# A new opening for a two-layer trunk kernel: sums of squares as columns, k tiles 0 to 2 in another order, tiles declared ahead

## The chip, the cores and the metric

The kernel runs on one core of one Trainium2 chip. It is one program for five engines: TensorE (PE; its weight loads are shown apart as PEld), VectorE (DVE), ScalarE (ACT), GpSimd (POOL) and SyncE (SP), which issues nearly all loads. The metric is device time in microseconds (us) of one execution, as a median over runs. A profiled execution has a span, from its first to its last instruction, and its own time, which also holds what lies around the span.

## The reference

Two layers work on 256 latent positions and 256 context positions, each 2048 wide, all in float32. Each layer normalises its input, scales and shifts it with vectors made from a conditioning vector, multiplies by one wide matrix, mixes three groups of columns in different ways, and multiplies by an output matrix. The opening of layer 0 is what matters here:

```python
def rmsnorm(x, g):
    xf = x.astype(jnp.float32)
    y = xf * lax.rsqrt(jnp.mean(xf * xf, axis=-1, keepdims=True) + EPS)
    return (y * g.astype(jnp.float32)).astype(x.dtype)

for l in range(DEPTH):
    shift, scale, gate = jnp.split(silu_c @ w_mod[l] + b_mod[l], 3, axis=-1)
    shift_c, scale_c, gate_c = jnp.split(silu_cc @ w_mod[l] + b_mod[l], 3, axis=-1)
    h = rmsnorm(x, g_pre[l]) * (1.0 + scale[:, None]) + shift[:, None]
    h_c = rmsnorm(ctx, g_pre[l]) * (1.0 + scale_c) + shift_c
    proj = h @ w_in[l]
    proj_c = h_c @ w_in[l]
    ...
```

## The kernel before

Latents and context lie side by side as 512 columns, and the 2048 features as 16 tiles of 128 partitions, the k tiles. For k tile 0 the order is: the sum of squares of the latents over all features, then its power -1/2, then that row spread over all partitions, then shift and scale of the tile (`mod_start`), then h for the latents (`make_h`), and only then the first products of the wide matrix. The context follows in the same steps while PE works on the latents.

A product in full precision is made of three in the fp32r form: weights and h are each split into a high part (a cast on ACT) and a low part (a subtraction on DVE), and `mm3` adds high x high, high x low and low x high. Weights come through three `raw` tiles and are split by `W.emitting(cut)` in pieces of `cut` columns, a cast and a subtraction for each; a load into a `raw` tile waits until the subtraction that read its old content is done. Tiles are handed out by tag, each tag with a fixed number of places that are used in turn.

The first sums (lines 1282 to 1300): ACT squares a loaded tile that holds two k tiles (128x512), PE multiplies it with 32 columns of ones (line 1286; four such products share one bank in four strips of partitions), ACT copies the 128x512 result (line 1291), four narrow products add the strips up and turn the row into columns (line 1295), DVE scales (line 465), POOL raises to the power (line 468), and `bcast` spreads it (line 489). `warm` issues idle matmuls (line 483).

`mod_start` makes shift and scale of one k tile: 16 products over 2 MB of loaded weights (line 169), a transpose on DVE (line 173), four small products (line 178, `modc`) and three small DVE instructions (lines 187 to 190). Its weights go by turns into two sets of tiles (mraw, macc, vv and mg, mgl, hh14 to hl15). `next(...)` and `mod_in` do one step of it, so the loop decides where each step stands. For each k tile the loop in `layer` issues four groups of av products (`start_av`; groups 0 and 1 are latents, 2 and 3 context) and two or three of au (`start_au`). Head 2 of au, called au2 here, has weights of its own, which stand in hh12, hl12, hh13 and hl13. Up to k tile EARLY the modulation of the next tile stands inside the iteration (early form); later tiles have it one tile further ahead, with modc right behind the 16 products (late form).

In this first stage the order on PE, DVE, ACT and SP is the order in which the code issues (`manual_schedule`); each engine works strictly through its list and waits where an operand isn't ready. SP's loads wait in the same way, for the tile they write to come free and for their turn.

Of the kernel before, what the change touches and what calls it, by code (L numbers as in the profile page):

```python
# [7 lines left out]
F32 = mybir.dt.float32  # L8
# [5 lines left out]
P = 128  # L14
# [52 lines left out]
def trunk_kernel(ctx: ExitStack, tc: tile.TileContext, xT, xhalf, cT, wss, wsl, wmod, win, wout0, wout1, const, vec, rows,  # L67
# [66 lines left out]
    gg0 = sb([P, KT, 2], F32, "gg0")  # L134
    g1 = []

    def mod_cols(l, cb, ps8):
# [145 lines left out]

    LOADS = [0, 2, 0, 2, 1, 1, 1, 1, 1, 0, 2, 0, 1, 1, 1, 0]
    SPLITS = [1, 1, 0, 2, 0, 1, 1, 1, 1, 1, 0, 2, 0, 1, 1, 1]
    EARLY = 7
    LOWC = 60
    YT = 3.0
    GATES = {2: 0, 14: 1}, {7: 2}, {12: 3}, {}
# [53 lines left out]
    class Stream:  # L343
# [247 lines left out]
    def layer(l):  # L591
# [43 lines left out]
        if l == 0:  # L635
# [8 lines left out]
            for k in range(KT):  # L644
                def take_in(n):
                    mod_in(k + 1, n)
# [8 lines left out]
                        mod_in(k + 1)  # L655
                        make_h(0, k + 1, rb0, [0, 1])

                if k == 2:
                    ws_[0] = ahead
                elif k % 2 == 0:  # L660
                    take(k)
                if 0 < k <= EARLY:
                    take_in(1)
                if k == 1:
                    next(state["load"])
                if k >= EARLY:
                    mod_in(k + 2, 1)
                for _ in range(LOADS[k]):
# [1 line left out]
                if k == 0:  # L670
# [3 lines left out]
                    au.extend(mm_ps("au") for _ in range(2))  # L674
                    take_in(2)
                    make_h(0, 0, rb0[:, CTX], [1])
                    take_in(1)
                    e = W.emitting(512)
                    next(e)
                    take_in(1)  # L680
                    next(e)
                    next(state["w0"])
                    start_av(0, (2,))
                    mod_in(1)
                    start_av(0, (3,))
                    make_h(0, 1, rb0, [0, 1], state["w0"])
                    take(0, (1,))
                    start_au(0, (0, 1))
                elif k == 1:
                    au.append(ms_ps("au"))  # L690
                    start_av(1, (0, 1))
                    take_in(5)
                    avs = W.emitting(512)
                    next(avs)
                    start_av(1, (2,))
                    take_in(1)
                    start_av(1, (3,))
# [553 lines left out]
    with tc.manual_schedule(engines={EN.PE}):  # L1251
# [27 lines left out]
        idle = mm_ps("idle")  # L1279
        rb0 = sb([P, T], F32, "acc")  # L1280

        def square(sq, s, i):
            q = w2k([P, T])
            A.activation(q, yo[2 * i + s], AF.Square)
            c = slice(32 * (i % 4), 32 * (i % 4) + 32)
            return lambda: PE.matmul(sq[c], ones[:, 0:32], q, start=i < 4, stop=i >= 4,
                                     tile_position=(0, 32 * (i % 4)))

        def sums_of(sq):
            row = w2k([P, T])  # L1290
            A.copy(row, sq)
            ps = ms_ps("rs")
            for j in range(2):
                for i in range(2):
                    PE.matmul(ps[:, j:j + 1], row[:, (2 * i + j) * P:(2 * i + j + 1) * P], cc("sel")[:, 0:1],
                              start=i == 0, stop=i == 1)
            return rstd_cols(ps[:, 0:2], 2, D)

        def spread(r, s):
            rb = bcast(r, 2)  # L1300
# [3 lines left out]
        for i in range(8):  # L1304
# [15 lines left out]
        warm(idle, 2)  # L1320
        sq = mm_ps("rs2")
        products = [square(sq, 1, i) for i in range(2)]
        list(m)
        warm(idle, 3)
        make_h(0, 0, rb0[:, LAT], [0])
        state["w0"] = e

        def context(between):
            products.extend(square(sq, 1, i) for i in range(2, 8))
            for p in products:  # L1330
                p()
            r = sums_of(sq)
            between()
            spread(r, 1)

# [83 lines left out]
```

## Time and profile before

| What | Value |
|---|---|
| Time, median of 3 runs | 1139.67 us (1139.26 to 1140.7) |
| Profiled execution, its own time | 1140.22 us |
| Its span | 1138.4 us |
| PE busy in the span | 1123.5 us, 99% |
| DVE, ACT, POOL busy | 880.6, 515.1, 34.6 us |
| Mean granted PE clock | 0.998 |

A row of the timeline gives start, length, engine, line, operation, output and inputs, shapes and a count of merged records; in brackets stands how long the engine had stood idle and what ended that. In a row of busy time by stretch each engine has its busy time and record count, in the order PE, PEld, DVE, ACT, POOL; then come the granted PE clock, the DMA engines' busy share and GB/s.

### The profile page before, as it was taken

The page shows a single profiled execution, that of the slowest core. Times are in us where ns is not written, and L with a number is a line of the kernel's source. Part 1 is how long each engine was busy: PE and PEld are TensorE (multiplying, and loading weights), DVE is VectorE, ACT ScalarE, POOL GpSimd, SP SyncE. Part 2 cuts the span into 40 slices and gives each one's busy share as a digit, 9 for nine tenths or more (in the row PEclk, how much of TensorE's full clock was granted, in tenths as well). Part 3 has the DMA queues.
Part 4 walks back from the last instruction along what each step waited for, and adds up shares of the span by engine and source line. Part 5 has one row for each costly group of instructions (what it writes and reads, how often), then busy time and mean ns, then how long its engine had stood idle before and what let it go on. Part 6 is the DMA issues. An engine that isn't in the chain of part 4 may idle for free.

```text
span 1138.4 us, 16831 instructions
## 1 busy us (share of the span) xinstructions
PE 1123.5 (99%) x6323; PEld 930.7 (82%) x6323; DVE 880.6 (77%) x1484; ACT 515.1 (45%) x938; POOL 34.6 (3%) x40
## 2 busy tenths in 40 slices
PE   8999999999999999999999999999999999999997
PEld 3667788888898888888888888988888988888885
DVE  1645499999987887789999994397788689868884
ACT  5322422222325667632533323365555369857551
POOL 0000000000000000000000000205000000000001
PEclk9999999999999999999999999999999999999999
DMA  9999756556655343355556665269656686555872
GB/s 351 404 379 405 254 187 189 176 194 212 212 167 185 111 136 117 116 188 186 165 190 215 213 197 162 63 187 236 209 179 210 213 274 193 175 164 191 294 260 74
DMA packets 72946, 234.28 MB, mean 206 GB/s; under 512 B 8480, under 2 KB 11424, under 8 KB 72864
## 3 DMA queue, kind: packets, MB, share of 16 engines
q1 hardware_dynamic: 70416, 231.10, 61.1%
q0 software_dynamic: 2304, 2.10, 1.2%
q8 instruction: 49, 0.80, 0.3%
q14 instruction: 33, 0.27, 0.1%
q10 hardware_dynamic: 144, 0.02, 0.0%
HBM read 231.08 MB, written 2.10 MB: 205 GB/s over the span
## 4 chain that ended last, share of the span: by engine, by line
PE 90%; DVE 5%; DMA 2%; ACT 1%; issue 1%; POOL 0%; SPq 0%; DVEq 0%; POOLq 0%; ACTq 0%
PE ps_t L437 13%; PE ps_t L439 13%; PE ps_t L438 13%; PE ps_t L559 10%; PE ps_t L560 5%; PE ps_y L437 3%; PE ps_y L439 3%; PE ps_y L438 3%; PE ps_mod L169 2%; PE ps_av L437 2%; DVE macc L207 2%; PE ps_av L438 2%; PE ps_av L439 2%; PE ps_tp L952 2%; PE ps_v L439 1%; PE ps_v L437 1%
## 5 line engine op out<-in xcount | busy, mean ns | idle before, releaser
L412 ACT CAST whi<-raw 128x1024 fp32r<-128x1024 f32 (+1 forms) x217 | 224.2, 1037 | 327.4 <-PE ps_t L438 186.4
L417 DVE TENSOR_TENSOR wlo<-raw,whi 128x1024 fp32r<-128x1024 f32 (+1 forms) x217 | 260.7, 1206 | 57.6 <-ACT whi L412 54.8
L437 PE MATMUL ps_t<-hh,whi 128*128 128x512 f32 (+1 forms) x704 | 268.6, 382 | 0.0
L439 PE MATMUL ps_t<-hh,wlo 128*128 128x512 f32 (+1 forms) x704 | 268.1, 381 | 0.0
L438 PE MATMUL ps_t<-hl,whi 128*128 128x512 f32 (+1 forms) x704 | 267.9, 381 | 0.0
L207 DVE SCALAR_TENSOR_TENSOR macc<-mraw,cs,macc 128x512 f32<-128x512 f32 x360 | 249.3, 746 | 17.9 <-DMA mraw<-in_wmod_dram 17.7
L559 PE MATMUL ps_t<-hh,whi 128*128 128x512 f32 x448 | 163.5, 402 | 0.0
L439 PEld LDWEIGHTS ps_t<-hh,wlo 128*128 128x128 f32 x704 | 132.3, 188 | 25.9
L437 PEld LDWEIGHTS ps_t<-hh,whi 128*128 128x128 f32 x704 | 132.5, 188 | 25.2 <-issue 0.8
L438 PEld LDWEIGHTS ps_t<-hl,whi 128*128 128x128 f32 x704 | 132.4, 188 | 24.1
L560 PE MATMUL ps_t<-hh,wlo 128*128 128x256 f32 x448 | 125.6, 280 | 0.0
L559 PEld LDWEIGHTS ps_t<-hh,whi 128*128 128x128 f32 x448 | 84.2, 188 | 19.0 <-issue 0.5
L560 PEld LDWEIGHTS ps_t<-hh,wlo 128*128 128x128 f32 x448 | 84.7, 189 | 0.5 <-issue 0.5
L525 ACT ACTIVATE hh<-w2k,sh 128x256 fp32r<-128x256 f32 x48 | 21.9, 502 | 76.4 <-DVE w2k L521 76.4
L437 PE MATMUL ps_y<-whi,hh 128*128 128x512 f32 x104 | 41.4, 398 | 0.0
L437 PE MATMUL ps_av<-whi,hh 128*128 128x512 f32 x96 | 40.0, 416 | 0.8 <-ACT hh L525 0.8
L439 PE MATMUL ps_y<-whi,hh 128*128 128x512 f32 x104 | 40.7, 392 | 0.0
L438 PE MATMUL ps_y<-wlo,hh 128*128 128x512 f32 x104 | 40.6, 390 | 0.0
L437 PE MATMUL ps_cx<-whi,hh 128*128 128x512 f32 x96 | 38.8, 404 | 0.0
L438 PE MATMUL ps_av<-wlo,hh 128*128 128x512 f32 x96 | 37.8, 393 | 0.0
L438 PE MATMUL ps_cx<-wlo,hh 128*128 128x512 f32 x96 | 37.4, 390 | 0.0
L454 ACT CAST w2k<-ps_tp 128x512 fp32r<-128x512 f32 x40 | 23.3, 583 | 23.2 <-PE ps_scc L438 12.7
(397 smaller groups left out, 1858.0 us busy)
## 6 DMA issues: line engine op xcount, KB each, us to landing
raw<-in_win_dram SPq DMA_DIRECT2D x158, 512.0 KB, 4.3
mraw<-in_wmod_dram SPq DMA_DIRECT2D x128, 512.0 KB, 4.4
raw<-in_wout_dram SPq DMA_DIRECT2D x60, 512.0 KB, 4.4
mraw<-in_wsl_dram SPq DMA_DIRECT2D x16, 512.0 KB, 7.1
yo<-in_xhalf_dram SPq DMA_DIRECT2D x16, 256.0 KB, 5.4
macc<-in_wsl_dram SPq DMA_DIRECT2D x8, 512.0 KB, 7.7
vv<-in_wsl_dram SPq DMA_DIRECT2D x8, 512.0 KB, 7.7
mg<-in_wsl_dram SPq DMA_DIRECT2D x8, 512.0 KB, 6.6
```

The source lines that it names most:

```text
L169: PE.matmul(ps[32 * kk:32 * kk + 32, 0:n], cpad[:, kg * 4 + kk], ws[kk], start=kg == 0, stop=kg == 3, tile_position=(0, 32 * kk))
L207: V.scalar_tensor_tensor(out=acc[:, s], in0=w[:, kk % 2], scalar=c, in1=acc[:, s], op0=ALU.mult, op1=ALU.add)
L412: A.copy(ph, rc)
L417: self.last = V.tensor_tensor(out=pl, in0=rc, in1=ph.bitcast(F32), op=ALU.subtract)
L437: PE.matmul(ps, st[0], mv[0], start=start, stop=False)
L438: PE.matmul(ps, st[0], mv[1], start=False, stop=False)
L439: PE.matmul(ps, st[1], mv[0], start=False, stop=stop)
L454: A.copy(hi, src)
L525: first = A.activation(h_of(l, k, sl)[0], t[:, sl], AF.Identity, bias=sh[l][:, k, s:s + 1])
L559: PE.matmul(ps, w[0], h, start=k == 0, stop=False)
L560: PE.matmul(ps[:, 0:S], w[1], h[:, 0:S], start=False, stop=k == KT - 1)
L952: PE.transpose(tp[:, (2 * j + b) * P:(2 * j + b + 1) * P], src, ident)
```

## The change

Four things change. The sums of squares no longer go through a row: the squares themselves are the weights, 128 columns at a time, against one column of ones, so that the result stands as columns at once; ACT's copy and the four products that followed it go. The order of PE's work is new up to k tile 2: three of the context's eight squares are summed ahead of the first av products, the five idle matmuls there go, part of tile 1's modulation stands between two av groups, au01's weights are split in quarters, au2's products for tiles 0 and 1 move from iteration 1 to iteration 2, and SP loads a slot earlier what au2 needs. EARLY is 8 instead of 7, so k tile 8 has the early form too. And tiles are declared once, in a fixed order, ahead of everything else, which sets where they lie in memory. Line numbers grow by 1 to 7 in the changed kernel.

```diff
+    for tag, n, bufs in (("join", 256, 2), ("w2k", 512, W2K), ("mraw", 1024, 2), ("macc", 1024, 1), ("vv", 1024, 1),
+                         ("raw", 1024, 3), ("rs_a", 4, 2), ("rs_b", 4, 2), ("acc", 512, 1), ("whi", 1024, 4),
+                         ("wlo", 1024, 4), ("hh0", 512, 1), ("hl0", 512, 1), ("mg", 1024, 1), ("mgl", 1024, 1)):
+        sb([P, n], F32, tag, bufs)
...
-    EARLY = 7
+    EARLY = 8
...
                     make_h(0, 0, rb0[:, CTX], [1])
+                    start_av(0, (2,))
                     take_in(1)
-                    e = W.emitting(512)
+                    take_in(1)
+                    e = W.emitting(256)
                     next(e)
-                    take_in(1)
                     next(e)
                     next(state["w0"])
-                    start_av(0, (2,))
+                    start_av(0, (3,))
                     mod_in(1)
-                    start_av(0, (3,))
...
                 elif k == 1:
-                    au.append(ms_ps("au"))
-                    start_av(1, (0, 1))
+                    next(state["load"])
+                    next(e)
+                    next(e)
+                    start_av(1, (0, 1, 2))
                     take_in(5)
                     avs = W.emitting(512)
                     next(avs)
-                    start_av(1, (2,))
+                    start_av(1, (3,))
                     take_in(1)
-                    start_av(1, (3,))
                     make_h(0, 2, rb0, [0, 1], avs)
-                    aus = W.emitting(256)
-                    next(aus)
-                    next(aus)
                     list(avs)
-                    list(e)
                     start_au(1, (0, 1))
-                    ahead = W.next()
+                elif k == 2:
+                    au.append(ms_ps("au"))
+                    start_av(2, range(nt))
+                    list(W.emitting(512))
                     ws_[2] = W.next()
                     start_au(0, (2,))
                     start_au(1, (2,))
-                elif k == 2:
-                    start_av(2, range(nt))
-                    list(aus)
                     take_in(5)
+                    list(e)
                     start_au(2, (0,))
...
-        def square(sq, s, i):
+        def square(ps, s, i):
             q = w2k([P, T])
             A.activation(q, yo[2 * i + s], AF.Square)
-            c = slice(32 * (i % 4), 32 * (i % 4) + 32)
-            return lambda: PE.matmul(sq[c], ones[:, 0:32], q, start=i < 4, stop=i >= 4,
-                                     tile_position=(0, 32 * (i % 4)))
+
+            def products():
+                if i == 0:
+                    PE.matmul(ps[:, 0:2], ones, zero4[:, 0:2], start=True, stop=False)
+                for j in range(4):
+                    PE.matmul(ps[:, j % 2:j % 2 + 1], q[:, j * P:(j + 1) * P], ones[:, 0:1], start=False,
+                              stop=i == 7 and j == 3)
+            return products
...
-        r0 = sums_of(sq)
+        r0 = rstd_cols(sq[:, 0:2], 2, D)
         e = W.emitting(512)
         next(e)
         next(e)
-        for _ in range(3):
-            next(m)
+        next(m)
+        next(m)
         spread(r0, 0)
         next(m)
         next(m)
-        warm(idle, 2)
+        next(m)
         sq = mm_ps("rs2")
-        products = [square(sq, 1, i) for i in range(2)]
+        products = [square(sq, 1, i) for i in range(3)]
         list(m)
-        warm(idle, 3)
+        for p in products:
+            p()
         make_h(0, 0, rb0[:, LAT], [0])
```

PE's list from k tile 0's modc to the end of the context's sums, before. In the names, modc is the small product of the modulation, idle the idle matmuls, av the first wide products, rs the sums, mod the modulation of k tile 1:

```order
L178 MATMUL ps_modc_234<-w2k_225,cst_79 32x4 x4
L483 LDWEIGHTS join_95
L483 MATMUL ps_idle_148<-join_95 128x512
...
L437 MATMUL ps_av_251<-whi_200,hh_69_245 128x512
...
L1286 MATMUL ps_rs_65_229<-w2k_230,ones_80 32x512
...
L1286 MATMUL ps_rs_65_229<-w2k_269,ones_80 32x512
L1295 MATMUL ps_rs_281<-cst_79,w2k_279 128x1 x4
L169 MATMUL ps_mod_290<-mg_130,kt_24_87 32x256 x4
```

The same stretch of PE's list now:

```order
L185 MATMUL ps_modc_279<-w2k_270,cst_79 32x4 x4
L1289 MATMUL ps_rs_90_272<-zero_22_84,ones_80 128x2
L1291 MATMUL ps_rs_90_272<-ones_80,w2k_273 128x1 x4
L1291 MATMUL ps_rs_90_272<-ones_80,w2k_275 128x1 x4
L1291 MATMUL ps_rs_90_272<-ones_80,w2k_277 128x1 x4
L444 MATMUL ps_av_306<-whi_245,hh_95_300 128x512
...
L1291 MATMUL ps_rs_90_272<-ones_80,w2k_314 128x1 x4
...
L1291 MATMUL ps_rs_90_272<-ones_80,w2k_338 128x1 x4
L176 MATMUL ps_mod_348<-mg_157,kt_24_87 32x256 x4
```

Eight wide products and four narrow ones behind the first av groups became 32 narrow ones, twelve of them ahead of av.

PE's list from the spread of the context's row (rb) to tile 0's first au product, before; hh and hl with two numbers are the modulation's weights of tile 1 in line 169, and h of tile 0 in lines 437 to 439:

```order
L489 MATMUL ps_rb_295<-identr_89,rs_b_288 128x128 x2
L169 MATMUL ps_mod_290<-mgl_132,kt_24_87 32x256 x4
L169 MATMUL ps_mod_290<-hh_40_134,kt_24_87 32x256 x2
L169 MATMUL ps_mod_290<-hl_41_136,kt_24_87 32x256 x2
L169 MATMUL ps_mod_290<-hh_42_138,kt_24_87 32x256 x2
L169 MATMUL ps_mod_290<-hl_43_140,kt_24_87 32x256 x2
L437 MATMUL ps_av_299<-whi_200,hh_69_245 128x512
...
L178 MATMUL ps_modc_329<-w2k_322,cst_79 32x4 x4
L437 MATMUL ps_av_300<-whi_200,hh_69_245 128x512
...
L437 MATMUL ps_au_301<-hh_69_245,whi_319 128x512
```

The same stretch now:

```order
L496 MATMUL ps_rb_353<-identr_89,rs_b_346 128x128 x2
L176 MATMUL ps_mod_348<-mgl_159,kt_24_87 32x256 x4
L176 MATMUL ps_mod_348<-hh_67_161,kt_24_87 32x256 x2
L176 MATMUL ps_mod_348<-hl_68_163,kt_24_87 32x256 x2
L444 MATMUL ps_av_357<-whi_245,hh_95_300 128x512
...
L176 MATMUL ps_mod_348<-hh_69_165,kt_24_87 32x256 x2
L176 MATMUL ps_mod_348<-hl_70_167,kt_24_87 32x256 x2
L444 MATMUL ps_av_358<-whi_245,hh_95_300 128x512
...
L185 MATMUL ps_modc_390<-w2k_380,cst_79 32x4 x4
L444 MATMUL ps_au_359<-hh_95_300,whi_382 128x512
```

The last two pieces of the modulation moved behind av group 2, and modc behind av group 3, with six au products between it and tile 1's av.

DVE's list from the splits of iteration 1 to the scale of k tile 3, before; wlo with raw_142 is the second half of au01, raw_367 is au2, and the transpose is tile 3's:

```order
L417 TENSOR_TENSOR wlo_396<-raw_365,whi_395 128x512
L417 TENSOR_TENSOR wlo_320<-raw_142,whi_319 128x512
L417 TENSOR_TENSOR hh_115_424<-raw_367,hh_113_422 128x256
L417 TENSOR_TENSOR hl_116_425<-raw_367,hl_114_423 128x256 x2
L173 STREAM_TRANSPOSE w2k_491<-ps_mod_474 128x256
L187 SCALAR_TENSOR_TENSOR gs_26_90<-ps_modc_496,vecs_78 128x2
```

The same stretch now, where raw_169 is au01 and raw_424 au2:

```order
L424 TENSOR_TENSOR wlo_458<-raw_422,whi_457 128x512
L424 TENSOR_TENSOR hh_144_516<-raw_424,hh_142_514 128x512
L424 TENSOR_TENSOR hl_145_517<-raw_424,hl_143_515 128x512
L180 STREAM_TRANSPOSE w2k_545<-ps_mod_528 128x256
L424 TENSOR_TENSOR wlo_383<-raw_169,whi_382 128x256 x2
L194 SCALAR_TENSOR_TENSOR gs_26_90<-ps_modc_554,vecs_78 128x2
```

The third and fourth quarters of au01 moved from ahead of tile 3's transpose to behind it. A load into that raw tile, the first of two that k tile 4 needs, waits for the fourth.

More of the change, by code (lines that the diff above doesn't have):

```diff
@@ L134, in trunk_kernel @@
     gg0 = sb([P, KT, 2], F32, "gg0")
+    for tag, n, bufs in (("join", 256, 2), ("w2k", 512, W2K), ("mraw", 1024, 2), ("macc", 1024, 1), ("vv", 1024, 1),
+                         ("raw", 1024, 3), ("rs_a", 4, 2), ("rs_b", 4, 2), ("acc", 512, 1), ("whi", 1024, 4),
+                         ("wlo", 1024, 4), ("hh0", 512, 1), ("hl0", 512, 1), ("mg", 1024, 1), ("mgl", 1024, 1)):
+        sb([P, n], F32, tag, bufs)
+    for k in (14, 15, 1, 12, 13, 2):
+        for x in "hl":
+            sb([P, T], F32, f"h{x}{k}")
     g1 = []
@@ L656, in h_next @@
                         make_h(0, k + 1, rb0, [0, 1])
-                if k == 2:
-                    ws_[0] = ahead
-                elif k % 2 == 0:
+                if k % 2 == 0:
                     take(k)
@@ L663, in layer @@
                     take_in(1)
-                if k == 1:
-                    next(state["load"])
                 if k >= EARLY:
@@ L1280, in trunk_kernel @@
         rb0 = sb([P, T], F32, "acc")
-        def square(sq, s, i):
+        def square(ps, s, i):
             q = w2k([P, T])
             A.activation(q, yo[2 * i + s], AF.Square)
-            c = slice(32 * (i % 4), 32 * (i % 4) + 32)
-            return lambda: PE.matmul(sq[c], ones[:, 0:32], q, start=i < 4, stop=i >= 4,
-                                     tile_position=(0, 32 * (i % 4)))
[L1289 to L1297, printed above, removed]
+            def products():
[5 more added lines that the diff above has]
+            return products
         def spread(r, s):
@@ L1328, in context @@
         def context(between):
[L1329 to L1332, printed above, removed]
+            for i in range(3, 8):
+                square(sq, 1, i)()
+            r = rstd_cols(sq[:, 0:2], 2, D)
             between()
```

## The prediction

> **What bounds the kernel now.** I read the page first, then busy time by stretch, then TensorE's, VectorE's and the DMA queue's timelines of the first 60 us, where every moved instruction stands.
>
> ```profile
> span 1138.4 us, 16831 instructions
> 0.00:20.00 20.00, 16.20 (x88) 5.66 (x89) 3.71 (x14) 10.82 (x20) 1.31 (x5) 1.00 0.92 331
> 20.00:40.00 20.00, 18.70 (x146) 10.68 (x145) 8.58 (x25) 9.21 (x20) 0.70 (x1) 1.00 1.04 401
> 40.00:60.00 20.00, 19.70 (x168) 12.71 (x167) 9.64 (x24) 4.45 (x8) 0.00 (x0) 1.00 1.03 405
> 60.00:120.00 60.00, 60.00 (x535) 41.86 (x534) 30.39 (x79) 14.98 (x27) 0.00 (x0) 1.00 1.01 392
> ```
>
> The first busy figure of a stretch is TensorE's (PE): after 20 us it stands still for 1.3 us, then 0.3 us, then never until 120 us. DMA is at its limit too, but PE hardly waits for it. So what this change adds to PE's own work behind 20 us lengthens the run one for one, and at most 1.6 us of waits can be won back there. Before 20 us PE mostly waits, for loads and for short chains:
>
> ```profile
> 1.90 2.74 PE L483 MATMUL ps_idle<-join 128*128 128x512 bf16 x6 [1.90 <-DVE join L1276]
> 4.57 3.68 PE L1286 MATMUL ps_rs<-w2k,ones 128*32 128x512 f32 x8
> 8.18 1.47 PE L483 MATMUL ps_idle<-join 128*128 128x512 bf16 x6
> 12.43 1.05 PE L1295 MATMUL ps_rs<-cst,w2k 128*128 128x1 f32 x8 [0.68 <-ACT w2k L1291]
> 15.31 0.71 PE L489 MATMUL ps_rb<-identr,rs_b 128*128 128x128 f32 x4
> 16.02 0.64 PE L169 MATMUL ps_mod<-vv,kt 128*32 128x256 f32 x8
> 17.33 0.24 PE L178 MATMUL ps_modc<-w2k,cst 128*32 128x4 f32 x8
> 19.17 0.50 PE L437 MATMUL ps_av<-whi,hh 128*128 128x512 f32 x1 [0.84 <-ACT hh L525]
> 20.80 2.81 PE L1286 MATMUL ps_rs<-w2k,ones 128*32 128x512 f32 x16
> 24.29 1.05 PE L1295 MATMUL ps_rs<-cst,w2k 128*128 128x1 f32 x8 [0.68 <-ACT w2k L1291]
> 26.38 0.71 PE L489 MATMUL ps_rb<-identr,rs_b 128*128 128x128 f32 x4 [0.47 <-POOL rs_b L468]
> ```
>
> An fp32 product leaves two records, so x8 are four products. The latents' sums are ready at 13.48, the context's at 25.34.
>
> **The new product's price.** A column product takes 128 columns of squares as weights and one column of ones. The same form stands late in the run, between other matmuls:
>
> ```profile
> 725.26 0.53 PEld L476 LDWEIGHTS ps_rs<-ones,acc 128*128 128x128 f32 x4
> 725.71 0.19 PEld L437 LDWEIGHTS ps_t<-hh,mraw 128*128 128x128 f32 x1
> 13.76 1.10 POOL L468 TENSOR_TENSOR rs_b<-rs_a,mhalf 128x2 f32<-128x2 f32 x1 [13.31 <-DVE rs_a L465]
> L1286 PE MATMUL ps_rs<-w2k,ones x5: 1057/1061/1062, 4.6 to 6.3; 128*32 128x512 f32 x5
> ```
>
> Four loads from 725.26 to 725.71 are 0.1125 us a pass, 0.225 a product, 0.9 for a tile's four. Each stream has 8 tiles: 32 products, 7.2 us, where before eight wide products, a copy on ScalarE (ACT) and four narrow ones stood.
>
> A, latents. The first idle set took 2.74 us and the second 1.47, and the five records up to 6.3 us last 1.06 where warm ones last 0.6: PE runs at half pace to about 7 us. The chain from 4.64: opening product, tile 0 at half pace 1.8, tile 1 mixed (to 7.9), two at 0.9, six idle matmuls 1.47, four at 0.9: sums at 14.8. From there to the spread (line 489) it takes 1.43, as in the rows (13.48, then POOL's 1.10 to 14.86, plus hand-overs), so 16.3. The order now puts the spread ahead of macc's and vv's products: 0.71 + 0.43 + 0.64 more, 18.1 against 16.66 before. A = +1.4. With loads at full pace throughout it is +0.1, since vv lands only at 16.0 anyway; at worst +1.6. I take the cold value, as the rows of that very time are cold. The Trainium skill, page "TensorE: Matmul & The Clock Gate", section "LDWEIGHTS (loading the stationary operand)", gives a load as columns over 1.2, an estimated 107 ns for 128, with no other figure for a cold clock. By that rule A would be +0.1 and the sum +3.4. No run here shows a cold 128-column fp32 load yet.
>
> B, first context tiles. Three tiles' products follow modc and stand ahead of the first av: modc 0.17 + opening 0.2 + 12 x 0.225 = 3.1 from modc's start, where av started 1.84 behind it (17.33 to 19.17) with idle matmuls as filler. B = +1.3 (1.0 to 1.5). ACT's third square ahead of hh costs nothing more: those products cover it. The five idle matmuls that go stood in waits: nothing.
>
> C, the other five. 20 x 0.225 = 4.5, plus av's 1.55: 6.1, against 6.1 before from 19.17 to 25.3 with copy and wait. C = 0 (-0.2 to +0.6, if each pass costs 0.12). The removed copy and its 0.68 wait pay for the longer products and no more. POOL's power and its 0.47 wait stay.
>
> **The order of k tiles 0 to 2.**
>
> ```profile
> 28.61 0.50 PE L437 MATMUL ps_av<-whi,hh 128*128 128x512 f32 x1
> 32.37 0.40 PE L439 MATMUL ps_av<-whi,hl 128*128 128x512 f32 x1
> 36.16 0.24 PE L178 MATMUL ps_modc<-w2k,cst 128*32 128x4 f32 x8
> 38.26 0.88 DVE L530 SCALAR_TENSOR_TENSOR hl<-w2k,sh,hh 128x256 fp32r<-128x256 f32 x2
> 38.64 0.50 PE L437 MATMUL ps_au<-hh,hh 128*128 128x512 f32 x1
> 39.52 0.50 PE L439 MATMUL ps_au<-hh,hh 128*128 128x512 f32 x1 [0.15 <-DVE hh L417]
> 40.56 0.39 PE L437 MATMUL ps_av<-whi,hh 128*128 128x512 f32 x1
> ```
>
> D. Half of tile 1's mod products (eight passes, 0.57 with the change of kind of matmul) moves behind the third av group: PE did them while it waited for hh; now it waits there and does them later, and each extra change between fp32 and fp32r costs 0.1. Then av of tile 1 follows modc after six au products, 0.17 + 1.48, and its first hl product is wanted 2.2 behind modc, while the rows from 36.16 to 38.26 + 0.44 show the first hl 2.5 behind it: 0.35 of wait. D = +1.2 (0.7 to 1.4) on the 3.76 from 28.61 to 32.37.
>
> E. Tile 2 has the same 0.35 wait, but au2's six products, which took 1.92 from 38.64 to 40.56 for 1.37 of work, come later and find their splits done: E = -0.3 (-0.6 to 0).
>
> ```profile
> 45.42 0.45 DVE L173 STREAM_TRANSPOSE w2k<-ps_mod 128x256 f32<-128x256 f32 x1 [3.74 <-PE ps_mod L169]
> 45.83 0.39 PE L439 MATMUL ps_au<-hh,wlo 128*128 128x512 f32 x1
> 39.05 0.42 DVE L417 TENSOR_TENSOR hh<-raw,hh 128x256 fp32r<-128x256 f32 x1
> ```
>
> F. VectorE's third quarter split of au01 now stands behind tile 3's transpose: ready at 45.42 + 0.37 + 0.42 = 46.2 on the old clock, wanted at 45.83. F = +0.4 (0.2 to 0.6).
>
> G. The fourth quarter is later still, and a load on SP's queue waits for its raw tile; so do all loads behind it, two of them split for tile 4 ahead of that tile's transpose.
>
> ```profile
> 49.32 1.04 ACT L412 CAST whi<-raw 128x1024 fp32r<-128x1024 f32 x1 [1.04 <-DMA raw<-in_win_dram]
> 50.40 2.58 DVE L417 TENSOR_TENSOR wlo<-raw,whi 128x1024 fp32r<-128x1024 f32 x2 [1.60 <-ACT whi L412]
> 53.40 0.25 PE L178 MATMUL ps_modc<-w2k,cst 128*32 128x4 f32 x8 [0.30 <-DVE w2k L173]
> raw<-in_win_dram SPq DMA_DIRECT2D x158, 512.0 KB, 4.3
> DMA to landing us min/median/max: 2.6/2.6/2.6
> ```
>
> modc already waits 0.30 here. With A to F all stands 4.0 later: the issue falls at about 50.2, the queue has run empty, and the load lands 3.3 later (the run's first load, 256 KB with nothing ahead, took 2.6, its last row above; 0.65 more for the second half) or 4.3 (the median). Second load 1.3 behind, cast 1.05, split 1.23, transpose 0.45: modc at 57.6 to 58.6 against 57.1 wanted. G = +0.4 (0 to 1.2).
>
> H. EARLY = 8 keeps tile 8 in the early form:
>
> ```profile
> 64.45 1.07 PE L169 MATMUL ps_mod<-mraw,kt 128*32 128x256 f32 x16
> 78.94 1.07 PE L169 MATMUL ps_mod<-mraw,kt 128*32 128x256 f32 x16
> 88.28 1.07 PE L169 MATMUL ps_mod<-mraw,kt 128*32 128x256 f32 x16
> 102.13 1.07 PE L169 MATMUL ps_mod<-mraw,kt 128*32 128x256 f32 x16
> ```
>
> Two early tiles take 14.49, two late ones 13.85: H = +0.3 (0.2 to 0.4). Its load order changes by one slot, ahead of products that all come later. The tiles declared ahead of time only move in memory; no row prices an address, I take nothing.
>
> Sum: 1.4 + 1.3 + 0 + 1.2 - 0.3 + 0.4 + 0.4 + 0.3 = +4.7. The profiled execution took 1140.22, which gives 1144.9; the median of the runs is 0.55 lower, so 1144.4. Ends summed: +1.4 to +7.3, 1141.1 to 1147.0.
>
> **Rivals.** One pass a product (not slower): if a product's second load hid behind the first, 0.112 each, then A and B are 0, and C is bound by five squares of 0.63 on ACT, -2.2; about 0.7 comes back because hl15's load lands only near 28; with D to H +2.0 it ends at +0.5, 1140.2. Between, the time passes +0.2% at about 0.16 us a product. Against it: both narrow groups in the rows pay two loads each.
>
> The reorder is free: VectorE's smaller splits come early enough and D to G vanish. Then A + B + H = +3.0, or with warm loads +1.7: 1141.4. For it: the pieces halve; against it: the modc chain above has no slack to give.
>
> The clock falls back: idle matmuls go and one-column products keep the array nearly empty from 11 to 22 us. Half pace for some 3.5 us there doubles twenty products: +4.5, 1149. Against it: PE's longest gap would be 0.6 us, and narrow groups before left the next products at full pace. The same page of the Trainium skill, "What's actually happening", halves the clock after an idle window of about 3.4 us; no gap in this trace is that long behind the start.
>
> **Chances.** Forecast 0.68, reorder free 0.10, one pass 0.10, clock 0.07, something unseen that gains 0.05. Within 0.2% (2.3 us, about what a measurement here can tell from none): one pass and half of "reorder free", 0.15; slower: the rest of these, 0.78; faster: 0.07, the unseen gain and a better end of one pass. The range 1140.4 to 1148.0 leaves out the faster cases and most of the clock's.
>
> **What would show it.** Right: line 1291 in after at 0.11 us a load; first spread near 16.3, first av near 22; context sums near 28; modc of tile 4 waiting for VectorE; from 60 us on every row later by one amount, 4 to 5 us. Wrong: a load pitch near 0.06, a first av by 20, or a shift that shrinks again after 120 us.

## The result, and the profile after

The changed kernel takes 1153.04 us (median of 6 runs, 1149.64 to 1160.39), the kernel before 1140.56 (6 runs, 1139.26 to 1142.42): 1.0114 times the time, 95% interval 1.008 to 1.0149. It is slower, as forecast, but by 12.5 us where 4.7 were forecast, and the range did not hold it. The profiled execution took 1153.92 us, its span is 1152.1.

The page's row of the granted clock, which was 9 in all 40 slices before, and the same stretches of the run as in the prediction:

```profile
span 1152.1 us, 16989 instructions
PEclk6799999999999999999999999999999999999999
0.00:20.00 20.00, 17.97 (x94) 13.79 (x94) 1.90 (x8) 7.26 (x13) 1.31 (x5) 0.70 0.92 333
20.00:40.00 20.00, 19.30 (x113) 16.72 (x110) 1.97 (x7) 5.04 (x10) 0.70 (x1) 0.59 0.69 267
40.00:60.00 20.00, 20.00 (x152) 12.02 (x155) 9.58 (x25) 6.51 (x15) 0.00 (x0) 0.95 0.59 224
```

TensorE (PE) is busier than before in the first 40 us (37.27 us against 34.90) and gets less done: its clock is 0.70 and 0.59 where it was 1.00. The transfers wait for it: from 20 to 60 us their share is 0.69 and 0.59, where before it was 1.04 and 1.03. PE's timeline shows where the time goes:

```profile
4.63 4.50 PE L1291 MATMUL ps_rs<-ones,w2k 128*128 128x1 f32 x32
9.00 2.72 PE L490 MATMUL ps_idle<-join 128*128 128x512 bf16 x6
11.51 6.83 PE L1291 MATMUL ps_rs<-ones,w2k 128*128 128x1 f32 x32
23.17 0.25 PE L185 MATMUL ps_modc<-w2k,cst 128*32 128x4 f32 x8 [0.68 <-DVE w2k L180]
23.59 3.95 PE L1291 MATMUL ps_rs<-ones,w2k 128*128 128x1 f32 x24
27.40 0.77 PE L444 MATMUL ps_av<-whi,hh 128*128 128x512 f32 x1
28.40 0.63 PE L446 MATMUL ps_av<-whi,hl 128*128 128x512 f32 x1
30.10 8.53 PE L1291 MATMUL ps_rs<-ones,w2k 128*128 128x1 f32 x40
39.66 1.22 PE L496 MATMUL ps_rb<-identr,rs_b 128*128 128x128 f32 x4
```

The second half of the latents' column products takes 6.83 us for 32 passes, 0.213 a pass; the context's last five tiles take 8.53 for 40, also 0.213. The forecast price was 0.1125. (A pass is one weight load of 128 columns with the product on it; an fp32 product makes two.) What stands between them is slow too: the second idle set takes 2.72 us (1.47 before), the context's spread 1.22 (0.71), an av product 0.63 (0.39). Cutting the run where the clock changes:

```profile
0.00:8.00 8.00, 5.97 (x36) 4.42 (x36) 1.13 (x6) 4.30 (x7) 0.20 (x4) 1.00 0.72 230
8.00:21.60 13.60, 13.60 (x68) 10.51 (x71) 0.77 (x2) 3.17 (x8) 1.10 (x1) 0.50 1.05 401
21.60:25.00 3.40, 2.73 (x39) 2.09 (x31) 1.34 (x6) 2.28 (x6) 0.00 (x0) 1.00 1.03 393
25.00:42.10 17.10, 17.07 (x84) 14.69 (x86) 1.11 (x3) 3.18 (x7) 0.70 (x1) 0.50 0.51 198
42.10:60.00 17.90, 17.90 (x140) 10.83 (x136) 9.10 (x24) 5.88 (x14) 0.00 (x0) 1.00 0.66 250
```

The clock is at half for 30.7 us in two stretches, and in both PE is busy for 13.60 of 13.60 and 17.07 of 17.10 us. It comes up at 21.6 us, 3.3 us behind the end of the latents' column products, for 3.4 us, and for good at 42.1, 3.5 us behind the end of the context's.

How far everything moved is read best from the group cx, whose first product starts near 149 us and its last near 817. Its row in a list of one tile's instructions, before and after (behind the count stand the shortest, median and longest duration in ns, then the first and the last start in us):

```profile
L437 PE MATMUL ps_cx<-whi,hh x96: 389/389/797, 149.4 to 816.8; 128*128 128x512 f32 x96
```

```profile
L444 PE MATMUL ps_cx<-whi,hh x96: 388/390/797, 164.9 to 830.5; 128*128 128x512 f32 x96
```

The changed kernel is 15.5 us late at the first and 13.7 at the second, which is also the difference of the spans (1152.1 against 1138.4). So there are two things to explain: 15.5 us instead of 4.7 at the end of the first stage, and 1.8 us that come back behind it.

### The profile page after: what moved, and what is told of

It reads as the page before. It is cut to its first block, busy times and chain, and to the rows that moved or that the text cites. A ratio compares the mean times of both kernels' runs of the same rounds, so it can differ in the third digit from the quotient of the medians.

```text
span 1152.1 us, 16989 instructions
## 1 busy us (share of the span) xinstructions
PE 1139.6 (99%) x6402; PEld 953.9 (83%) x6402; DVE 880.8 (76%) x1484; ACT 513.2 (45%) x936; POOL 34.6 (3%) x40
## 4 chain that ended last, share of the span: by engine, by line
PE 90%; DVE 5%; DMA 2%; issue 1%; ACT 1%; POOL 0%; SPq 0%; DVEq 0%; POOLq 0%; ACTq 0%
PE ps_t L444 13%; PE ps_t L446 12%; PE ps_t L445 12%; PE ps_t L566 10%; PE ps_t L567 5%; PE ps_mod L176 3%; PE ps_y L444 3%; PE ps_y L446 3%; PE ps_y L445 3%; DVE macc L214 2%; PE ps_av L444 2%; DMA mraw<-in_wmod_dram 2%; PE ps_av L445 2%; PE ps_av L446 2%; PE ps_rs L1291 2%; PE ps_tp L953 2%
```

## The experiments

Theory "gate": the clock goes by how much PE streams (the columns that pass through the array), not by whether it stands still; one-column products are no work to it. Rivals: the price of 0.213 us belongs to the 128-column fp32 load itself; or the new order costs it. The second question is what gives time back late in the run. Of each kernel the ratio is to the kernel before on the same chip.

### Wide ones: the changed kernel with 128 columns of ones

```
-    PE.matmul(ps[:, 0:2], ones, zero4[:, 0:2], start=True, stop=False)
+    PE.matmul(ps[:, 0:256], wz[:, 0:P], wz[:, 0:256], start=True, stop=False)
...
-    PE.matmul(ps[:, j % 2:j % 2 + 1], q[:, j * P:(j + 1) * P], ones[:, 0:1], start=False,
+    PE.matmul(ps[:, j % 2 * 128:j % 2 * 128 + 128], q[:, j * P:(j + 1) * P], ones[:, 0:128], start=False,
```

The same sums, 128 times over; one column of each 128 is read.

> The changed kernel with 128 columns of ones instead of one in each column product; the sums and everything else stay. Theory 'gate' (TensorE's clock goes by how much streams through the array, and one-column products count as idle): granted clock 1.00 from about 7 us on, 0.11 us a weight load, first av near 22 us, time 1143.5 to 1146. Rival 'price' (a product that takes fresh squares as weights is slow by itself, and the clock record follows from it): loads at 0.21 us for most of the first 40 us, time 1150 to 1160 as in the changed kernel.

Measured: 1141.21 us (10 runs, 1140.29 to 1142.46), ratio 1.0004, interval 0.9995 to 1.0013. PE's timeline:

```profile
9.77 1.46 PE L490 MATMUL ps_idle<-join 128*128 128x512 bf16 x6
11.07 3.73 PE L1291 MATMUL ps_rs<-ones,w2k 128*128 128x128 f32 x32
18.61 0.25 PE L185 MATMUL ps_modc<-w2k,cst 128*32 128x4 f32 x8 [0.66 <-DVE w2k L180]
18.91 2.84 PE L1291 MATMUL ps_rs<-ones,w2k 128*128 128x128 f32 x24
21.51 0.47 PE L444 MATMUL ps_av<-whi,hh 128*128 128x512 f32 x1
22.97 4.63 PE L1291 MATMUL ps_rs<-ones,w2k 128*128 128x128 f32 x40
28.63 0.71 PE L496 MATMUL ps_rb<-identr,rs_b 128*128 128x128 f32 x4 [0.47 <-POOL rs_b L475]
30.87 0.50 PE L444 MATMUL ps_av<-whi,hh 128*128 128x512 f32 x1 [0.52 <-ACT hh L532]
```

Its clock in the two stretches where the changed kernel's was at half:

```profile
8.00:21.60 13.60, 12.50 (x126) 10.33 (x125) 2.58 (x8) 6.47 (x15) 1.10 (x1) 1.00 1.04 399
25.00:42.10 17.10, 16.11 (x138) 10.07 (x136) 6.57 (x21) 3.92 (x9) 0.70 (x1) 1.00 0.83 313
```

32 passes in 3.73 us and 40 in 4.63: 0.116 each, for passes that do 128 times the arithmetic of those that take 0.213 in the changed kernel. The weight loads, the order, the declarations are the same. The whole loss of 12 us hung on the clock, and the clock on the width of the products. The 0.213 us is therefore no fixed price of a 128-column load, which the rival had it for. The time is some 2 us below the 1143.5 that theory "gate" gave at best, since that sum held nothing that comes back late.

### Sums only: the kernel before with the column products alone

```
-        r0 = sums_of(sq)
+        r0 = rstd_cols(sq[:, 0:2], 2, D)
...
-            r = sums_of(sq)
+            r = rstd_cols(sq[:, 0:2], 2, D)
```

with the new products of the diff above in square; order, idle matmuls and buffers stay as before.

> The kernel before with only the sums as columns; order of k tiles, idle matmuls, EARLY 7 and places as before. If the sums carry the loss: granted clock 0.5 to 0.8 between 10 and 40 us, context spread 8 to 13 us later than the 26.4 of before, time 1147 to 1155. If the loss needs the idle matmuls' removal or the new order too: clock near 1.0, time 1141 to 1144.

Measured: 1151.54 us (4 runs, 1150.91 to 1154.44), ratio 1.0095, interval 1.0077 to 1.0114. The second half of the latents' column products, and the stretches by its clock:

```profile
14.06 3.77 PE L1290 MATMUL ps_rs<-ones,w2k 128*128 128x1 f32 x32
14.40:17.70 3.30, 3.30 (x31) 3.30 (x30) 0.00 (x0) 0.00 (x0) 0.00 (x0) 1.00 1.04 394
17.70:21.20 3.50, 3.50 (x29) 1.75 (x29) 0.77 (x2) 0.00 (x0) 1.10 (x1) 0.51 1.06 394
21.20:31.40 10.20, 9.23 (x78) 7.21 (x77) 1.81 (x6) 5.16 (x10) 0.00 (x0) 1.00 1.04 400
31.40:41.60 10.20, 10.17 (x59) 6.85 (x58) 2.15 (x5) 1.91 (x4) 0.70 (x1) 0.50 0.28 110
```

The column products alone lose 11 us and bring the half clock along, with the five idle matmuls still in their waits. The order is not needed for it. The row of the products shows one thing more: these 32 one-column passes, which follow six idle matmuls, run at full pace (0.118 us), and the half clock comes only behind them, for 3.5 us in which hardly any column product stands. So the slow pace belongs to the clock and not to the products, and the clock comes down only some time after such products begin: 3.6 us here, 5.1 us in the context, whose 64 passes begin at 26.26.

### Order only: the changed kernel with the sums of before

```
-        r0 = rstd_cols(sq[:, 0:2], 2, D)
+        r0 = sums_of(sq)
...
-            r = rstd_cols(sq[:, 0:2], 2, D)
+            r = sums_of(sq)
```

and the wide row products of before in square.

> The changed kernel with the sums of the kernel before (wide products, copied row, narrow products): new order, EARLY 8, no five idle matmuls, tiles declared ahead. Theory 'gate': clock 1.00 as before, only the prediction's terms D to H remain, +1 to +3, time 1141.5 to 1143.5. Rival (order or missing idle matmuls carry a large part): clock under 0.9 somewhere in 10 to 40 us, or time over 1146.

Measured: 1139.57 us (10 runs, 1138.3 to 1141.41), ratio 0.9986, interval 0.9976 to 0.9995. Its cx row:

```profile
L444 PE MATMUL ps_cx<-whi,hh x96: 389/389/797, 151.8 to 815.8; 128*128 128x512 f32 x96
```

The rest of the change is no loss at all: 2.4 us late at the first cx product (149.4 before), it is 1.0 us early at the last (816.8 before). Something gains 3.4 us in between, which again puts the time below what theory "gate" gave (1141.5 at least). The clock was not 1.00 throughout, as I had expected: the trace has one stretch at half clock, from 14.9 to 18.3 us. By its clock alone that is the rival's sign, but it is a single stretch, which the kernel with the declarations alone shows too (below), and the loss did not come with it.

### One and three idle products a tile, 32 and 64 columns

The first two put idle 512-column matmuls behind each tile's four column products:

```
                 for j in range(4):
                     PE.matmul(ps[:, j % 2:j % 2 + 1], q[:, j * P:(j + 1) * P], ones[:, 0:1], start=False,
                               stop=i == 7 and j == 3)
+                warm(idle, 1)
```

(warm(idle, 3) in the second). The other two are the wide-ones kernel with 32 and with 64 columns in place of 128.

> The changed kernel with one idle bf16 matmul of 512 columns behind each tile's four column products (16 more, 0.22 us each at full clock). Theory 'gate': PE's streamed share rises from near 0 to about a fifth; if that is enough the clock stays near 1.0 and the time falls to 1145 to 1149 in spite of 3.5 us more work; if not, the clock stays at 0.5 to 0.7 and the time is 1153 to 1160. Rival 'price': 1156 to 1158.

> The changed kernel with three idle 512-column products after each tile's column products, where one a tile left the clock at half until 48 us. They stream about 0.64 us beside 0.45 us of column products at full clock: three fifths of the time. If the clock goes by the share of time in which columns are streamed, this share holds the clock up: the granted clock is at 1.0 in all stretches after 10 us but one at most, the products cost 16 x 0.64 = 10.2 us where nothing covers them, some 3 us of the latents' half lie beside the loads, and the time is about 1149 us (1146 to 1152). If each return of one-column products closes the gate however much stands between them, the clock stays at half to past 50 us and the time is over 1165 us.

> The changed kernel with 32 columns of ones in each column product in place of one (128 kept the clock at full speed, one did not). If the clock goes by the share of time in which columns are streamed, a pass of 0.11 us with 32 columns (32/2.4 = 0.013 us of streaming by the 0.213 us that 512 columns take at full clock elsewhere in the trace) streams an eighth of the time, less than the run with one idle product a tile, which fell to half: half clock here too, from 8 to about 40 us, and about 1152 us. If any width of some tens of columns counts as work: full clock from 8 us and 1141 us.

> The changed kernel with 64 columns of ones in each column product. 128 columns kept the clock at full speed, 32 left it at half until 47 us, and three 512-column idle products between each four one-column products (three fifths of the time in streaming, estimated) left it at half too. If what counts is the share of the time in which columns are streamed and the border lies above three fifths, 64 columns, half of what 128 stream in the same 0.11 us pass, are too few: half clock until 40 us or later and 1150 to 1158 us. If the border lies between 32 and 64 columns a product, the clock is full from about 8 us and the time is 1141 us.

Measured: one idle product 1158.47 us (4 runs, 1154.45 to 1161.17, ratio 1.0139, interval 1.0111 to 1.0167); three 1167.22, 32 columns 1157.59, 64 columns 1146.31 (one run each). Passes by PE's timeline, with three idle products, with 32 columns, with 64:

```profile
18.62 1.71 PE L1291 MATMUL ps_rs<-ones,w2k 128*128 128x1 f32 x8
35.80 1.03 PE L1291 MATMUL ps_rs<-ones,w2k 128*128 128x1 f32 x8
39.72 1.71 PE L1291 MATMUL ps_rs<-ones,w2k 128*128 128x1 f32 x8
46.33 0.95 PE L1291 MATMUL ps_rs<-ones,w2k 128*128 128x1 f32 x8
```

```profile
13.89 6.88 PE L1291 MATMUL ps_rs<-ones,w2k 128*128 128x32 f32 x32
34.41 8.58 PE L1291 MATMUL ps_rs<-ones,w2k 128*128 128x32 f32 x40
```

```profile
4.54 7.04 PE L1291 MATMUL ps_rs<-ones,w2k 128*128 128x64 f32 x32
13.76 3.68 PE L1291 MATMUL ps_rs<-ones,w2k 128*128 128x64 f32 x32
27.16 4.61 PE L1291 MATMUL ps_rs<-ones,w2k 128*128 128x64 f32 x40
```

With 32 columns every pass runs at half pace (0.215 to 0.22 us). With 64 the first 32 do (0.22) and the latents' other 32 and the context's last 40 run at full pace (0.115), but one more stretch, from 23.8 to 27.2 us, is at half clock, with six av products in it. The start is slow with 128 columns too, though for less long (the same 32 passes took 5.29 us there, 7.04 with 64). So, by one run each, the width at which this stretch keeps its clock lies between 32 and 128, and 64 keeps it only in part; its time agrees with neither of the two that I had expected. One idle product a tile fits the half clock of theory "gate" (1153 to 1160) and does not tell it from rival 'price' (1156 to 1158). The cure by idle matmuls is worse than the disease: three a tile are slow to 34 us, fast, slow again near 40 and fast from 45 on, and cost more than they save. My expectation there had the share wrong: four column products are eight passes, 0.95 us and not 0.45, beside some 0.7 us of idle products (six of them took 1.46 above), so the share was some two fifths and not three. What exactly the gate counts, and where it tips, stays open; that the same pattern was slow near 40 us and fast at 46 shows that one run's share does not settle it.

### What comes back late: declarations or order

First the kernel before with the block of declarations and nothing else:

```
+    for tag, n, bufs in (("join", 256, 2), ("w2k", 512, W2K), ("mraw", 1024, 2), ("macc", 1024, 1), ("vv", 1024, 1),
+                         ("raw", 1024, 3), ("rs_a", 4, 2), ("rs_b", 4, 2), ("acc", 512, 1), ("whi", 1024, 4),
+                         ("wlo", 1024, 4), ("hh0", 512, 1), ("hl0", 512, 1), ("mg", 1024, 1), ("mgl", 1024, 1)):
+        sb([P, n], F32, tag, bufs)
+    for k in (14, 15, 1, 12, 13, 2):
+        for x in "hl":
+            sb([P, T], F32, f"h{x}{k}")
```

> The kernel before, with the block of tile declarations put in and nothing else; every instruction and its order stay, only the places of the tiles in memory change. Theory 'places': the steady fall of the shift between 240 and 700 us (from +1.53 to -0.07 us against the kernel before in the run with the new order and the old sums, from +15.4 to +13.8 us in the changed kernel, flat at +11.64 us in the run with the column sums alone, which has no declarations) comes from where the tiles lie, so this kernel starts as before to within 0.1 us up to 200 us, then gains 1.4 to 1.7 us by 700 us: 0.12 to 0.15% faster, 1139.2 us against 1140.8. Theory 'order' (the fall comes from what the new beginning leaves behind, such as which slot of a rotating buffer is next): this kernel is level with before from the first to the last stage, ratio 1.000 within 0.0005.

And the order-only kernel without this block:

> The changed kernel with the sums of before (wide row products, a copy, column products from the row) and without the block of tile declarations: the new order of tiles 0 to 2 and the later change of form alone. Theory 'places': +2.2 to +2.6 us against before at 60 to 180 us, as with the declarations, then no steady fall between 240 and 700 us; what is left is the two steps near 220 and 735 us that the run with the column sums alone shows too (-0.2 and -0.9 us), so +1.2 us at the end, ratio 1.001. Theory 'order': the shift falls steadily as with the declarations and the end comes 0.8 to 1.0 us earlier than before, ratio 0.999.

Measured: declared only 1139.74 us (12 runs, 1136.58 to 1142.32), ratio 0.9986, interval 0.9975 to 0.9997; order undeclared 1141.21 (11 runs, 1139.69 to 1142.54), ratio 1.0001, interval 0.9991 to 1.0011. The cx row and the long stage in both, declared first:

```profile
L444 PE MATMUL ps_cx<-whi,hh x96: 389/389/797, 150.3 to 816.4; 128*128 128x512 f32 x96
240.00:700.00 460.00, 459.95 (x2279) 388.10 (x2278) 401.79 (x625) 190.92 (x346) 0.00 (x0) 1.00 0.55 176
```

```profile
L437 PE MATMUL ps_cx<-whi,hh x96: 389/389/797, 150.7 to 817.6; 128*128 128x512 f32 x96
240.00:700.00 460.00, 460.00 (x2271) 386.77 (x2271) 401.59 (x624) 190.86 (x346) 0.00 (x0) 1.00 0.55 176
```

The same stretch of the kernel before, and the waits of its PE behind 120 us:

```profile
240.00:700.00 460.00, 460.00 (x2272) 386.80 (x2271) 400.60 (x623) 190.86 (x346) 0.00 (x0) 1.00 0.55 176
PE ps_rb L489 <- POOL rs_b L468: 0.7, 1, 0.7
PE ps_z L438 <- DVE w2k L455: 0.4, 1, 0.4
```

PE is busy throughout that stage in all three, at full clock, and in its 460 us the declared kernel does 2279 matmul records, the two undeclared ones 2272 and 2271: seven or eight more, at 0.23 us each 1.6 to 1.8 us. From the first cx product to the last the declared one gains 1.3 us on the kernel before (it is 0.9 us late at the first, since one stretch of 3.4 us near 26 us ran at half clock in this profile, and 0.4 early at the last); the undeclared one gains 0.5, of which 0.4 is a wait that it does not have. The medians alone would not settle it: the second interval holds the 1.001 of theory 'places', but its lower end lies only just above the 0.999 of theory 'order'. The traces of all kernels do. Between the first and the last cx product, with each kernel's own late waits set aside, those without the block (order undeclared, sums only, EARLY 8 below) gain 0.1 to 0.2 us on the kernel before, and those with it 1.6 to 2.7. So the places of the buffers in memory, with no instruction changed, are worth 1.3 us by the medians (0.14%, interval 0.03 to 0.25%) and 1.8 us by that count. Which place matters and why is not shown; the wide products of the stage last about 1 ns less in the mean (391, 390 and 391 ns for their three lines before, 390, 389 and 390 with the declarations).

The other part are the two waits. In the wide-ones kernel PE waits for nothing behind 120 us, where the kernel before waits 0.7 and 0.4 us. It is not shown what decides them: a first stage that ends later does not do it by itself, since the changed kernel, whose first stage ends latest of these, still shows both (0.7 and 0.3), and the one with the declarations alone waits 0.8 twice.

### The form of the tiles: EARLY

The kernel before with EARLY 8; the same with the declarations and EARLY 5; and with EARLY 3:

```
-    EARLY = 7
+    EARLY = 8
```

> The kernel before with EARLY 8 for 7 and nothing else. By the prediction's term +0.3 us from tile 8 on (tile 7 in the earlier form, in which its products wait for VectorE about 0.33 us longer), and the same +0.3 us at the end, ratio 1.0003. If instead the tile's form is what lets the changed kernel catch up after 200 us, the end comes earlier than before: ratio 0.999.

> The kernel before with the block of tile declarations and the change of form at tile 5 (EARLY 5 for 7). Two effects that should add: the declarations gave -0.5 us at the end of the trace and -1.3 us in the medians (-1.5 us between 240 and 700 us); the later form took about 0.33 us more a tile in the traces when EARLY went up by one, so two tiles fewer should give -0.7 us by 60 us. Together -2.0 us: 1139.0 us against 1141, ratio 0.998. Rival: the operations of the following tiles' modulation that the later form issues a tile further ahead do not have their weights yet (the loads are what bounds the stage), so tiles 5 and 6 wait for transfers, the 0.7 us is gone, and the ratio is 0.9986 as with the declarations alone, or above it.

> As the kernel with EARLY 5, but EARLY 3, the lowest that the code's branches for tiles 0 to 2 leave. If the later form saves 0.33 us a tile whatever the tile: -1.3 us from it and -1.3 us from the declarations, 1138.4 us, ratio 0.9977. If the loads bound the stage from here: raw tiles for the modulation two tiles ahead are asked for before they have landed, VectorE waits for them at tiles 3 to 5, and the time is level with before or up to 2 us over it.

Measured: EARLY 8 1140.59 us (10 runs, 1139.64 to 1141.04), ratio 1.0002, interval 0.9993 to 1.0011; declared with EARLY 5 1138.46 (12 runs, 1136.8 to 1140.48), ratio 0.9981, interval 0.9971 to 0.9991; declared with EARLY 3 1142.58 (10 runs, 1141.04 to 1145.44), ratio 1.0027, interval 1.0018 to 1.0036. The first moves nothing that can be told from no change; in its trace the first cx product starts 0.3 us later than before, as expected. The second has the lowest ratio of this study, but its interval holds the 0.9986 of the declarations alone, so the times do not show that the tile form and the places add. In the traces, which both have a stretch at half clock near 26 us, its first cx product starts 0.9 us before that of the declarations alone (149.4 against 150.3), which fits the 0.7 us expected. The third, 2.7 us over the kernel before and so beyond the 2 us of its rival, shows the price of going too far:

```profile
PE ps_modc L185 <- DVE w2k L180: 4.9, 1, 4.9
```

With EARLY 3 the modulation of tile 4 is wanted 4.9 us before its weights have passed through VectorE (before: 0.3 us in all). It is the wait that the prediction looked for at that place, brought about by another edit. Here PE does stand idle, and behind it too the clock is low: 0.93 from 40 to 60 us and 0.90 from 60 to 80, about 7 us at half.

## Why the prediction was right and wrong

**The sign** was right, but in good part by luck. I expected the change to be slower because its products cost more passes and its order costs waits. Where the clock stays up, those costs come (+4.2 us at the first cx product), and still the time is level with before (1.0004). What makes the changed kernel slower is the clock, which I had given a chance of 0.07. **The size** failed in the terms A, B and C, all by one step: the price of a column pass, taken as 0.1125 us from products that stand between wide matmuls at 725 us. It was 0.213, and the neighbours of these products went at half pace with them. Measured against the rows of before:

| term | forecast | changed kernel | wide ones, full clock |
|---|---|---|---|
| A, to the first modc (17.33) | +1.4 | 23.17: +5.8 | 18.61: +1.3 |
| B, modc to the first av (1.84) | +1.3 | 4.23: +2.4 | 2.90: +1.1 |
| C, first av to the context's spread (19.17 to 26.38) | 0 | 12.26: +5.1 | 7.12: -0.1 |
| all, at the first cx product (149.4) | +4.7 | 164.9: +15.5 | 153.6: +4.2 |

The last column is what the prediction described: with the clock held up, its three terms come out within 0.25 us each. So the counting of instructions was sound; the clock under them was not.

**The clock rival was dismissed by the wrong rule.** I gave it 0.07 and +4.5 us, for some 3.5 us at half pace between 11 and 22 us. It was the mechanism, but for 13.6 us from 8 us on and for another 17.1 from 25 us on, which the rival left out altogether. The step that failed is "Against it: PE's longest gap would be 0.6 us". The longest gap behind the start was indeed about that (0.68, the wait of the first modc), in the two slow stretches PE was busy for all but 0.03 us of the 30.7, and the clock fell all the same. The Trainium skill, page "TensorE: Matmul & The Clock Gate", section "What's actually happening", speaks of an idle window of about 3.4 us. The stretches here fit its length (the single ones are 3.3 to 3.5 us), but here windows full of one-column products were treated like idle ones. The rows that I held against the rival, narrow products with full pace behind them, were groups of about 1 us, too short to fill such a window.

**The price of a load.** By the same page of the Trainium skill, "LDWEIGHTS (loading the stationary operand)", columns over 1.2, a load of 128 columns is an estimated 107 ns, and the prediction let that rule stand beside the row. The 0.116 us at full clock are near it, the 0.213 at half are not.

**A's cold start** was right in kind: the first 32 passes took 4.50 us in the changed kernel and 5.29 with wide ones, where 3.6 would be full pace. The error was that PE would stay at full pace from about 7 us on: in the changed kernel it did so until 8.

**The reorder, D to H,** was forecast at +2.0 in all. In the wide-ones kernel it is 4.2 less 2.3 (30.87 against 28.61 at the spread's next av), so +1.9, and of its parts G and E were wrong. The first hl product of tile 1, a product of au01 and the modc of tile 4 with wide ones, and in the changed kernel two loads and au01's last two quarters:

```profile
35.91 0.50 PE L446 MATMUL ps_av<-whi,hl 128*128 128x512 f32 x1
49.82 0.49 PE L446 MATMUL ps_au<-hh,wlo 128*128 128x512 f32 x1 [0.24 <-DVE wlo L424]
57.38 0.25 PE L185 MATMUL ps_modc<-w2k,cst 128*32 128x4 f32 x8 [0.19 <-DVE w2k L180]
```

```profile
55.63 1.53 SPq L390 DMA_DIRECT2D raw<-in_win_dram  x2
60.93 0.72 DVE L424 TENSOR_TENSOR wlo<-raw,whi 128x256 fp32r<-128x256 f32 x2
```

D: from 30.87 to 35.91 are 5.04 us, where 28.61 to 32.37 were 3.76 before, so +1.3 against +1.2. F: the product at 49.82 waits for the third quarter and starts 0.64 behind its neighbour instead of 0.23, so +0.4 as forecast. G, forecast at +0.4, did not happen: the wait of modc at tile 4 is 0.19 us and was 0.30. Its premise was wrong, also where the change is described: the two loads that tile 4's splits read are issued at 55.63 and behind it, 5 us ahead of the third and fourth quarters' splits at 60.93, so they wait for neither. In the changed kernel no wait stands at that modc at all. At it the shift is 4.0 (57.38 against 53.40), 1.7 more than at 30.87; less D, F and G this leaves +0.1 for E, where -0.3 was forecast. H is too small to be told from no change in the times (EARLY 8 alone: ratio 1.0002), and +0.3 as forecast in that kernel's trace.

**"Every row later by one amount" from 60 us on** was wrong: 1.8 us came back by 817 us in the changed kernel and 3.8 in the wide-ones kernel (4.2 late at the first cx product, 0.4 at the last). I had listed a shrinking shift as a sign of error and had no term for it; "no row prices an address, I take nothing" is the step that missed up to 1.8 us of it, all but 0.1 of what came back in the changed kernel. In the wide-ones kernel the two late waits that did not come are 1.1 us more, and the remainder of about 1 us was not traced.

So the change itself, with its products wide enough to hold the clock, is neither faster nor slower than before (1.0004), because a first stage some 4 us longer meets gains of nearly the same size later; and its declarations alone are worth keeping.

## What to carry to other kernels

Before putting many small products in place of few wide ones, look at how much they stream, not only at how long they take: a stretch of some 4 us or more of one-column products can halve TensorE's clock for itself and its neighbours while the profile shows TensorE fully busy. Read the granted clock of the stretch (and the pass time of a known instruction there) before pricing anything by rows from elsewhere in the run; if narrow products are wanted, streaming 128 columns instead of one cost nothing here. And a shift measured early need not reach the end: compare a known instruction early and late in the run, and look for what gains or waits in between.

## What the runs showed of the hardware that was not expected

- A pass that streams 128 columns behind a 128-column fp32 load takes 0.116 us; the same load with one column, in the same place, 0.213, since it does not keep the clock up. Where the clock is still up, that takes 0.118.
- The records of the clock leave out a slow start: with 32 columns the stretch of 10 to 20 us is given as full clock although every pass in it takes 0.215 us, and the mean over the run is given as 0.997. The longest of the changed kernel's six runs (1160.39 us) also has a recorded mean of 0.998, the others 0.984 to 0.991. The pace of known instructions has to be read beside it:

```profile
10.00:20.00 10.00, 10.00 (x44) 8.53 (x43) 0.00 (x0) 1.16 (x2) 0.00 (x0) 1.00 1.04 401
```

- Moving buffers in memory alone changes the pace of a stage in which TensorE is never idle, by seven records in 2272 (0.3%).
